# Channel shuffle by tiles: the order of the small tiles at the start and at the end

## Chip, cores, metric

One core of one Trainium2 chip. Times are device microseconds (us) of one execution. Unless said otherwise they are medians of executions in the undisturbed (fast) state. A transfer is issued by an instruction and lands when its completion is signalled. A packet is one record of the trace's DMA view; for the tiles here it is one partition's row, so a tile is 128 packets, 8 on each of 16 DMA engines.

## The reference, cut

```python
def reference(x, groups):                  # x: float32 (16, 64, 64, 256), groups: 8
    b, h, w, c = x.shape
    x = x.reshape(b, h, w, groups, c // groups)
    x = x.transpose(0, 1, 2, 4, 3)         # swap (8, 32) to (32, 8) in each pixel
    return x.reshape(b, h, w, c)
```

65,536 pixels of 1 KB are read and written, 67.11 MB each way. Nothing is computed.

## The kernel before

The pixels are cut into 24 tiles. A tile of q has q KB on each of 128 partitions. Each is loaded, shuffled by one VectorE copy and stored; loads go out on one DMA queue, stores on another.

```python
_SIZES = [4, 4, 8] + [24] * 20 + [16]      # KB a partition
_IN_BUFS = 4
_OUT_BUFS = 4
# ... (pools, flat views of x and out)
    first = 0
    for q in _SIZES:
        in_tile = in_pool.tile([P, biggest * c], F32, name="in_tile")
        nc.sync.dma_start(out=in_tile[:, : q * c], in_=rows(x_flat, first, q))
        out_tile = out_pool.tile([P, biggest * c], F32, name="out_tile")
        nc.vector.tensor_copy(
            out=out_tile[:, : q * c].rearrange("p (i j g) -> p i j g", j=CPG, g=G),
            in_=in_tile[:, : q * c].rearrange("p (i g j) -> p i j g", g=G, j=CPG),
        )
        nc.scalar.dma_start(out=rows(out_flat, first, q), in_=out_tile[:, : q * c])
        first += P * q
```

## Time and profile before

| | before |
|---|---|
| time, first three runs | 317.67 us (317.63 to 317.87) |
| span in the profile | 315.2 us |
| VectorE busy | 122.2 us, 39% |
| rate of both queues, 40 to 280 us | 433 GB/s |

The prediction below shows the page's shares, the rate by stretch and the copies by shape. Two more views of the kernel before belong to the argument. First the DMA issues: transfer, issuing queue, number, KB each, median us from issue to landing.

```profile
in_tile<-in_x_dram SPq DMA_DIRECT2D x20, 3072.0 KB, 52.3
out_dram<-out_tile ACTq DMA_DIRECT2D x20, 3072.0 KB, 40.1
```

A 3 MB transfer alone would need 3.146 MB / 433 GB/s = 7.3 us. These take 52 and 40, so each queue holds several transfers at all times. Second, the end of the chain of waits: start, duration, what.

```profile
244.21 49.91 DMA in_tile<-in_x_dram
...
294.24 3.86 DVE out_tile L49
```

### The profile page before, as it was taken

What the parts mean: (1) busy time and instruction counts of PE and PEld (TensorE: products, weight loads), DVE (VectorE), ACT (ScalarE), POOL (GpSimd) and SP (SyncE); (2) the same over time, 40 slices, a digit from 0 to 9 for tenths busy, and PEclk for the clock granted to TensorE, in tenths of its full rate; (3) what the DMA queues carried; (4) which work ended last, traced back from release to release, by engine and by line L of the source; (5) the groups of instructions that cost most, each with busy time, mean ns of one, the idle gap of its engine ahead of it and who ended that gap; (6) DMA issues with size and microseconds to landing.
All of it is one profiled execution on the core that took longest, in us unless ns stands there. A gap on an engine that the chain in (4) does not pass through costs nothing.

```text
span 315.2 us, 178 instructions
## 1 busy us (share of the span) xinstructions
DVE 122.2 (39%) x24; POOL 0.2 (0%) x4
## 2 busy tenths in 40 slices
DVE  2277517070625335260707162442517070625400
POOL 0000000000000000000000000000000000000000
DMA  8999999999999999999999999999999999999997
GB/s 316 399 458 407 423 424 446 430 421 446 437 415 446 437 418 443 440 415 443 440 415 443 443 412 443 446 409 443 446 415 437 446 415 437 443 420 431 431 437 319
DMA packets 6912, 134.22 MB, mean 426 GB/s; under 512 B 768, under 2 KB 768, under 8 KB 1280
## 3 DMA queue, kind: packets, MB, share of 16 engines
q1 hardware_dynamic: 3456, 67.11, 49.9%
q10 hardware_dynamic: 3456, 67.11, 49.5%
HBM read 67.11 MB, written 67.11 MB: 426 GB/s over the span
## 4 chain that ended last, share of the span: by engine, by line
DMA 38%; another core or an unknown queue 30%; DVE 25%; issue 0%; DVEq 0%
DMA in_tile<-in_x_dram 38%; DVE out_tile L49 25%; DVEq L49 0%
## 5 line engine op out<-in xcount | busy, mean ns | idle before, releaser
L49 DVE COPY out_tile<-in_tile 128x6144 f32<-128x6144 f32 (+3 forms) x24 | 122.2, 5093 | 175.9 <-DMA in_tile<-in_x_dram 175.7
L71 POOL MEMSET const-bfloat16-1.0<- 128x1 bf16 x1 | 0.1, 101 | 0.0
L71 POOL MEMSET const-uint8-127<- 128x1 uint8 x1 | 0.1, 101 | 0.0
L71 POOL MEMSET const-float32-0.0<- 128x1 f32 x1 | 0.1, 98 | 0.2 <-issue 0.2
L71 POOL MEMSET const-float32-1.0<- 128x1 f32 x1 | 0.1, 98 | 0.0
## 6 DMA issues: line engine op xcount, KB each, us to landing
in_tile<-in_x_dram SPq DMA_DIRECT2D x20, 3072.0 KB, 52.3
out_dram<-out_tile ACTq DMA_DIRECT2D x20, 3072.0 KB, 40.1
in_tile<-in_x_dram SPq DMA_DIRECT2D x1, 2048.0 KB, 49.9
out_dram<-out_tile ACTq DMA_DIRECT2D x1, 2048.0 KB, 16.3
in_tile<-in_x_dram SPq DMA_DIRECT2D x2, 512.0 KB, 3.8
in_tile<-in_x_dram SPq DMA_DIRECT2D x1, 1024.0 KB, 6.2
out_dram<-out_tile ACTq DMA_DIRECT2D x2, 512.0 KB, 16.8
out_dram<-out_tile ACTq DMA_DIRECT2D x1, 1024.0 KB, 27.1
```

What stands on the lines that cost most here:

```text
L49: nc.vector.tensor_copy(out=out_tile[:, : q * c].rearrange("p (i j g) -> p i j g", j=CPG, g=G), in_=in_tile[:, : q * c].rearrange("p (i g ...
L71: nc = _bacc.Bacc("TRN2", target_bir_lowering=False, num_devices=1)
```

## The change

The intent is to give the last tile less work after its load (a short copy, a short store), and to grow the first tiles evenly.

```diff
-_SIZES = [4, 4, 8] + [24] * 20 + [16]
+_SIZES = [4, 8, 16] + [24] * 20 + [4]
```

## The prediction

> **What bounds the kernel now.** I read the page first (shares, slices, queues), then the groups by shape, the stretches of DMA rate, the landing times of single transfers, and last the chain. From the page:
>
> ```profile
> span 315.2 us, 178 instructions
> DVE 122.2 (39%) x24; POOL 0.2 (0%) x4
> ...
> DMA  8999999999999999999999999999999999999997
> ...
> DMA packets 6912, 134.22 MB, mean 426 GB/s; under 512 B 768, under 2 KB 768, under 8 KB 1280
> q1 hardware_dynamic: 3456, 67.11, 49.9%
> q10 hardware_dynamic: 3456, 67.11, 49.5%
> ```
>
> VectorE works 39% of the span, the DMA engines all of it but the first and last slice. Queue q1 carries the loads, q10 the stores, 67.11 MB each. How steady that is shows in the busy times by stretch (us, VectorE, POOL, clock, DMA share, GB/s):
>
> ```profile
> 0.00:2.00 2.00, 0.00 (x0) 0.20 (x4) 1.00 0.20 45
> 2.00:8.00 6.00, 2.30 (x3) 0.00 (x0) 1.00 1.05 400
> 8.00:40.00 32.00, 18.32 (x4) 0.00 (x0) 1.00 1.00 422
> 40.00:280.00 240.00, 92.05 (x17) 0.00 (x0) 1.00 1.00 433
> 280.00:294.00 14.00, 5.71 (x1) 0.00 (x0) 1.00 1.00 431
> 294.00:313.00 19.00, 3.86 (x1) 0.00 (x0) 1.00 1.00 432
> 313.00:316.00 3.00, 0.00 (x0) 0.00 (x0) 1.00 0.13 55
> ```
>
> The rate is 433 GB/s with both queues at work (40 to 280) and 432 with stores alone (294 to 313): one ceiling, whoever uses it. 134.22 MB / 0.4327 MB per us = 310.2 us of the 315.2. The five left: 1.73 before the first packet, 1.15 from the last packet (314.08) to the end of the span, and about 2.2 of stalls. Only those 2.2 could depend on this change.
>
> The chain of waits names loads (38%), the copy (25%) and an unknown queue (30%). That is a trap: it follows semaphores, and a load's landing is late because its packets share a full pipe. It also ends at the last copy (298.1) and does not show the 16 us of stores after it. The wait of VectorE for loads (175.7 us) is idle time of an engine that is not the bound.
>
> **What the Trainium skill says.** (1) "DMA: Bandwidth & Descriptors", section "Where 436 GB/s comes from", gives a ceiling of 435.2 GB/s; its warning there lets HBM traffic bind at about 358. The trace has 433 between HBM and SBUF, so here the higher figure binds, and the measurement decides. (2) The same page, "Queues, rings and completion order": each DMA engine takes turns between the rows that have work, packet by packet. The trace agrees, and that is the key to the tail (below). (3) The same page, section "SWDGE vs HWDGE vs iDMA", says packets are preferably at most 4096 B. The packet records here disagree: one packet is one partition's row, 4096 to 24,576 bytes, on both queues.
>
> **The change part by part.** The sizes before are 4, 4, 8, twenty of 24, 16; after 4, 8, 16, twenty of 24, 4. That is the same multiset: one 4 goes from second to last, the 16 from last to third. Nothing is added or removed, 24 loads, 24 copies, 24 stores remain, and so do buffers and waits in kind. Instruction order in the built kernel confirms it. So two sums can't change.
>
> VectorE, from the groups by shape:
>
> ```profile
> L49 DVE COPY out_tile<-in_tile 128x6144 f32<-128x6144 f32 x20 | 114.2, 5708 | 163.7 <-DMA in_tile<-in_x_dram 163.7
> L49 DVE COPY out_tile<-in_tile 128x4096 f32<-128x4096 f32 x1 | 3.9, 3861 | 6.5 <-DMA in_tile<-in_x_dram 6.5
> L49 DVE COPY out_tile<-in_tile 128x1024 f32<-128x1024 f32 x2 | 2.2, 1094 | 4.3 <-DMA in_tile<-in_x_dram 4.1
> L49 DVE COPY out_tile<-in_tile 128x2048 f32<-128x2048 f32 x1 | 2.0, 2019 | 1.4 <-DMA in_tile<-in_x_dram 1.4
> ```
>
> 114.2 + 3.9 + 2.2 + 2.0 = 122.2 us before and after, far under the span.
>
> DMA: undisturbed packets occupy an engine 155 ns for 4 KB, 305 for 8, 607 for 16, 908 for 24 (packet records, start to start). A tile is 128 rows, so 8 packets on each of 16 engines. Per engine and direction: 2 x 8 x 0.155 + 8 x 0.305 + 8 x 0.607 + 160 x 0.908 = 2.48 + 2.44 + 4.86 + 145.28 = 155.06 us; both directions 310.1. Same after.
>
> What does move is who is served when. Because turns go by packet and every tile is 8 packets, loads and stores advance tile for tile, whatever their size. A small packet beside a large one gets a small share. Check on the last load of before, 16 KB packets beside 24 KB stores: 8 x (0.607 + 0.908) = 12.12 us; it landed 12.13 after the load before it. A 4 KB store beside 24 KB loads: 8 x 1.063 = 8.5; the second store landed 8.56 after the first. The lead of loads over stores, counted in packets, is thus fixed when stores begin. Before, the first store was issued at 5.26, its first packet went at 9.29, by when an engine had taken about 26 load packets. When the loads end, 26 store packets per engine remain, 8 of the last tile (16 KB) and 18 of 24 KB: 18 x 0.908 + 8 x 0.607 = 21.2 us. The last load packet ended at 292.86; 292.86 + 21.2 = 314.06, and the last store packet ended at 314.08. The last store's issue and its time from issue to landing show the same queue:
>
> ```profile
> L53 ACTq DMA_DIRECT2D out_dram<-out_tile x1: 338/338/338, 298.1 to 298.1; - x1
> DMA to landing us min/median/max: 16.3/16.3/16.3
> ```
>
> It was issued at 298.1 and landed 16.3 later, of which its own 2.10 MB take 4.86. The copy of 3.86 us before it lay wholly under stores already queued. So before has no exposed tail but the drain itself.
>
> After, start: the first tile is the same, so the first copy ends near 5.2 and the first store is issued near 5.26. By then loads of 4, 8, 16 and 24 KB are queued: 52 KB x 128 = 6.8 MB, 15.8 us of work, against 40 KB and 12.1 us. The fifth load is issued at 5.25 as before. No gap. Load 2 lands near 6.6, its copy (2.02) ends near 8.7; load 3 near 12, its copy (3.86) near 16. Stores take 6.1 us (4 KB beside 16 KB), 9.7 (8 beside 24) and 12.1 (16 beside 24), so each next one is issued before the last is done. Stores begin after about 19 to 21 load packets (estimate: the same four packets, or the same four us, after issue).
>
> After, end: the lead is about 20 packets, not 26. The last load (4 KB packets beside 24 KB stores) takes 8 x 1.063 = 8.5 us. Then 12 store packets of 24 KB and 8 of 4 KB remain: 10.9 + 1.2 = 12.1 us. So the last load lands near 302, its copy of 1.09 ends near 303.5, and the last store, with up to 4 us to its first packet, is ready by 307.5. The stores ahead of it run to about 312.7. It is hidden with 5 us to spare. Sum: path 310.1 before, 310.1 after; difference 0, but for stalls.
>
> Stalls: the packet records show about 0.5 us lost in the first packets, 0.45 at 7 to 9 where loads go to 24 KB packets while no store runs, 0.35 at 31 to 37, and up to 0.7 at the end where the slowest of 16 engines trails the first. The new order may save the second, as stores will run before loads turn to 24 KB. I take 0.2 off, a choice, within what I can't know (0.5 either way). 317.67 - 0.2 = 317.5.
>
> **The rivals.** First, the intended gain: last copy 3.86 to 1.09 and last store 4.86 to 1.24 us, together 6.4, giving 311.3 (just 2% faster). For it: the copy is last in the chain of waits. Against: 16.3 us from issue to landing, so the copy is not exposed, and the bytes taken off the last store are only moved earlier. Second, the tail turns into a new wait: the last load is starved to a seventh of the pipe, the store queue runs dry before it lands, and 1.1 of copy, about 1.4 of issue and receipt (0.73 to 1.73 at the first load, 314.08 to 314.43 at the last store) and 1.2 of store are exposed, 3.7 in all: about 321.4. Against: 12 us of stores should be queued. It would need the lead to fall by more than ten packets. Third, a start that is starved by longer early tiles, or out buffers that come free late: some 2 to 4 us more. Against: the queue of loads is deeper, and the store lag shrinks, so buffers come free earlier. Fourth, small packets being dearer in company: their number is unchanged.
>
> **Range and chances.** Runs of before lie within 0.24 us, and stalls may move by 0.5; so 316.7 to 318.3 holds it 8 times in 10. Within 2% (311.3 to 324.0) is 98%; both sides 1% each, for a rival at its full size.
>
> **What would show it.** Right: 1280 packets under 8 KB again and VectorE at 122.2 us; 432 to 433 GB/s from 40 to past 310; a median landing time of loads still 52.3 us (four tiles of 14.54 less the copy), of stores down from 40.1 to about 31 (20 x 1.816 less 5.8, estimate); the last load landing between 299 and 305, and the last store 8 to 13 us after its issue. Wrong: a dip in the last slices before the last store, or a span that falls by more than 1 us with the same rate. The first would say that the packet lead did not hold; the second that stalls of engines, not bytes, had set the end.

## The result and the profile after

| | before | after |
|---|---|---|
| median of 6 runs | 317.72 us (317.00 to 317.87) | 316.94 us (316.87 to 317.08) |
| span in the profile | 315.2 us | 315.3 us |

The ratio is 0.9979, interval 0.9966 to 0.9992: 0.2% faster. A ratio here is the mean time of one kernel's fast runs over that of the other's of the same rounds, so not quite the ratio of the medians.

The two spans do not show the 0.2%. The profiled execution of before took 317.02 us, as little as the fastest of the six timed ones; that of after took 317.08, the slowest of its six. A profile is one execution; where a kernel scatters, look up which one it was. The experiments take this up.

The page after:

```profile
span 315.3 us, 178 instructions
DVE 122.0 (39%) x24; POOL 0.2 (0%) x4
...
DMA  8999999999999999999999999999999999999997
...
DMA packets 6912, 134.22 MB, mean 426 GB/s; under 512 B 768, under 2 KB 768, under 8 KB 1280
```

The packet line is identical, 1280 under 8 KB included: the multiset of packets has not changed. The stretches after (us, VectorE, POOL, clock, DMA share, GB/s):

```profile
0.00:2.00 2.00, 0.00 (x0) 0.20 (x4) 1.00 0.18 31
2.00:8.00 6.00, 2.44 (x2) 0.00 (x0) 1.00 1.02 410
8.00:40.00 32.00, 15.92 (x4) 0.00 (x0) 1.00 1.01 421
40.00:280.00 240.00, 91.81 (x17) 0.00 (x0) 1.00 1.00 433
280.00:294.00 14.00, 5.12 (x2) 0.00 (x0) 1.00 0.99 427
294.00:313.00 19.00, 6.68 (x2) 0.00 (x0) 1.00 1.00 428
313.00:316.00 3.00, 0.00 (x0) 0.00 (x0) 1.00 0.25 102
```

The pipe is as full as before, start and end included. (The view counts a packet in the stretch where it starts. With its bytes spread over its duration, 280 to 312 us loses 0.05 us, and 0.04 before: 427 and 428 are no dip.) What moved is the order in it. The DMA issues after:

```profile
in_tile<-in_x_dram SPq DMA_DIRECT2D x20, 3072.0 KB, 52.3
out_dram<-out_tile ACTq DMA_DIRECT2D x20, 3072.0 KB, 31.2
```

Loads take as long as before, stores 9 us less, because they begin 5 packets earlier in the order of loads. Nine us of latency less on each of 20 stores, and nothing of it in the time. The end of the chain after:

```profile
256.08 46.27 DMA in_tile<-in_x_dram
...
302.47 1.10 DVE out_tile L49
```

The last copy is 2.8 us shorter and ends 5.5 us later (303.6 against 298.1). The last store after, issue and time to landing:

```profile
L53 ACTq DMA_DIRECT2D out_dram<-out_tile x1: 339/339/339, 303.6 to 303.6; - x1
DMA to landing us min/median/max: 10.9/10.9/10.9
```

It lands 10.9 us after issue, of which its 0.52 MB need 1.24. The rest it waits behind other stores.

### The profile page after: what moved, and what is told of

It is laid out like the page before. It is cut to its first block, busy times and chain, and to the rows that moved or that the text cites. A ratio compares the mean times of both kernels' runs of the same rounds, so it can differ in the third digit from the quotient of the medians.

```text
span 315.3 us, 178 instructions
## 1 busy us (share of the span) xinstructions
DVE 122.0 (39%) x24; POOL 0.2 (0%) x4
## 2 busy tenths in 40 slices
DMA packets 6912, 134.22 MB, mean 426 GB/s; under 512 B 768, under 2 KB 768, under 8 KB 1280
## 4 chain that ended last, share of the span: by engine, by line
DMA 36%; another core or an unknown queue 33%; DVE 26%; SPq 0%; issue 0%; DVEq 0%
DMA in_tile<-in_x_dram 36%; DVE out_tile L49 26%; SPq L47 0%; DVEq L49 0%
## 5 line engine op out<-in xcount | busy, mean ns | idle before, releaser
L49 DVE COPY out_tile<-in_tile 128x6144 f32<-128x6144 f32 (+3 forms) x24 | 122.0, 5082 | 181.6 <-DMA in_tile<-in_x_dram 181.6
## 6 DMA issues: line engine op xcount, KB each, us to landing
in_tile<-in_x_dram SPq DMA_DIRECT2D x20, 3072.0 KB, 52.3
out_dram<-out_tile ACTq DMA_DIRECT2D x20, 3072.0 KB, 31.2
```

The source lines that it names most:

```text
L49: nc.vector.tensor_copy(out=out_tile[:, : q * c].rearrange("p (i j g) -> p i j g", j=CPG, g=G), in_=in_tile[:, : q * c].rearrange("p (i g ...
```

## The experiments

All twelve kernels give the reference's result. Where a stall is sized below ("lost"), it is the length of a stretch less the bytes that the packet records put in it (each packet's spread evenly over its duration) over 432.7 GB/s.

### 1. Is the 0.2% real, and is it the start or the end?

**null_before**: the kernel before, unchanged.

```diff
 (no edit)
```

> The kernel before against itself. Theory (bytes at a fixed rate, the rest small stalls): 317.0 to 317.9 us, ratio 1.000 within 0.001; VectorE 122.2 us; last store 16.3 us from issue to landing. If the run before's two levels (317.0 once, 317.6 to 317.9 otherwise) are chance of one execution, both levels show again, and the 0.2% of the changed kernel is real only if its runs stay at 317.0. Rival: the 0.2% is noise between chips or rounds, then this null ratio leaves 1.000 by about 0.002 as well.

Measured: 317.63 us (317.22 to 317.85, 5 runs), ratio 0.9996 (0.9984 to 1.0009). The null does not leave 1, and three more kernels below repeat the 0.9978 in two rounds; the 0.2% is not noise between rounds. The scatter of 0.6 us is the kernel's own.

**start_only** and **end_only**: one half of the change each.

```diff
-_SIZES = [4, 4, 8] + [24] * 20 + [16]
+_SIZES = [4, 4, 8, 16] + [24] * 20           # start_only
+_SIZES = [4, 8] + [24] * 20 + [16, 4]        # end_only
```

> Sizes 4, 4, 8, 16, twenty of 24: the 16 leaves the end, the 4 stays at the start. Theory: same bytes, same packets, 316.8 to 317.9 us; lead of loads about 27 packets, so the last load lands near 290 and the last store of 24 KB takes about 20 us from issue to landing. Rival (exposed tail): last copy 5.7 instead of 3.9 us and last store 7.3 instead of 4.9, together 4.2 us more, 321.9. Rival (start sets the 0.2%): 317.0 or 317.7 according to whether the stall sits in the second 4 KB tile.

> Sizes 4, 8, twenty of 24, 16, 4: the 4 goes to the end, the 16 stays next to it. Theory: 316.8 to 317.9 us, last load lands 302 to 306, last store hidden behind the 16 KB one. Rival (exposed tail): 2.8 us of copy and 3.6 us of store less, 311.3. Rival (last load starved to a seventh of the pipe and then exposed): 321.4.

Measured: start_only 317.65 us (317.34 to 317.88), ratio 0.9998 (0.9986 to 1.0011); its last load landed at 293.2, three later than expected, its last store took 16.0 from issue to landing where about 20 was expected. The last copy and store were 4.2 us longer in sum than before and the time did not move, against 321.9 for an exposed tail. end_only 316.95 us (316.93 to 317.10), ratio 0.9978 (0.9966 to 0.9991); last load at 306.4, just past the 302 to 306 expected. Not 311.3 and not 321.4. Both rivals about the tail miss by 4 us or more.

But end_only shows the 0.2%. It differs in two things, though: no second 4 KB tile at the start, and 4 KB at the end. So they were crossed, in the next round.

**start_48_end_16** and **start_44_end_8**:

```diff
-_SIZES = [4, 4, 8] + [24] * 20 + [16]
+_SIZES = [4, 8] + [24] * 10 + [4] + [24] * 10 + [16]   # start_48_end_16
+_SIZES = [4, 4, 16] + [24] * 20 + [8]                  # start_44_end_8
```

> Sizes 4, 8, ten of 24, 4, ten of 24, 16: start of the changed kernel, end of the kernel before. The four kernels so far fall in two groups, 316.9 to 317.1 (start 4, 8; last tile 4) and 317.2 to 317.9 (start 4, 4, 8; last tile 16 or 24). Theory S (the start sets it: with two 4 KB tiles first, the third load's first packets stall at 4 to 6 us, where the profile of the repeated kernel before has 227 GB/s against 410 after the change): 316.9 to 317.1, rate of 4 to 6 us near 410. Theory E (the end sets it, the 16 engines end more evenly on 4 KB packets): 317.4 to 317.9.

> Sizes 4, 4, 16, twenty of 24, 8: start of the kernel before, small last tile. Theory S: 317.2 to 317.9 with a scatter of 0.3 us or more between runs, rate of 4 to 6 us well under 400 in a profile of a slow run. Theory E: 316.9 to 317.2 with little scatter.

Measured: start_48_end_16 317.00 us (316.97 to 317.12), ratio 0.9978 (0.9964 to 0.9991). start_44_end_8 317.79 us (317.29 to 318.28), ratio 1.0001 (0.9989 to 1.0014). The start sets it, not the end. The four kernels that begin 4, 8 with nothing else altered in copies or buffers (the changed one, end_only, start_48_end_16, and queue_warm below) have 21 runs within 316.87 to 317.12, whatever tile is last; the three experiments with four buffers that begin 4, 4 with all loads on one queue have 15 runs from 317.22 to 318.28. The kernel before was also run beside each round: with the first six, 33 runs from 317.00 to 318.05, two of which (317.00, 317.09) lie among the fast group. So the start 4, 4, 8 costs about 0.7 us in most executions and next to nothing in a few.

A candidate for what stalls shows from 4 to 6 us, the columns as above (in so short a stretch the last two are rough). The repeated kernel before, in its profiled execution of 317.22 us:

```profile
4.00:6.00 2.00, 1.41 (x2) 0.00 (x0) 1.00 1.09 227
```

The kernel before, in its profiled execution of 317.02 us:

```profile
4.00:6.00 2.00, 1.74 (x2) 0.00 (x0) 1.00 1.05 428
```

The changed kernel:

```profile
4.00:6.00 2.00, 1.10 (x1) 0.00 (x0) 1.00 1.01 410
```

The same program had 227 GB/s here in one execution and 428 in another. In the first, the packet records show the two 4 KB loads through near 4.5 us on most engines, and then the first 8 KB packets of the third load taking 1.1 to 1.7 us on 12 of the 16, where 0.309 is normal: 1.0 us lost from 4 to 6 us. start_only lost 0.43 there in a run of 317.65; its longest 8 KB packet took 0.99, and five took over half as long again as normal. start_44_end_8 lost 0.19 in a run of 317.29, the fastest of its five, so it does not confirm the stall, and my expectation of a rate well under 400 for a slow run stayed untested. The kernels that begin 4, 8 lost 0.07 to 0.12.

This does not yet explain the times. The profile with the 1.0 us stall is of the fastest run of its five, 0.2 us over the run of before that has no stall: it lost less afterwards. By 40 us the profiles of the three 4, 4 experiments had lost 1.9 to 2.1 us in all, those of the four 4, 8 kernels 1.7 to 1.8, that of before 1.6; from 312 us to the last packet all lost 0.2 to 0.7 more, start_only (0.7) the most, as the engines do not end together (its last packets end between 313.6 and 314.7). So the place of the 0.7 us is shown, the start; that it is this stall is not.

The DMA share stays at 1.09 in the stalled stretch: a stalled packet counts as busy. The rate tells, the share doesn't.

**third_load_moved** (third round): sizes as before, the third load issued first on the other queue.

```diff
+    def load(k):                        # cut; the plain loop goes
+        ...
+        queue = nc.scalar if k == 2 else nc.sync
+        queue.dma_start(out=tiles[k][:, : q * c], in_=rows(x_flat, firsts[k], q))
+
+    for k in range(_IN_BUFS):
+        load(k)          # the first four loads ahead of all stores
```

> The kernel before (sizes unchanged) with the third load (8 KB) issued first on the queue that issues the stores, so it does not stand behind the two 4 KB loads. If the 0.7 us of the start order 4, 4, 8 come from that load not being ready when the first 1.05 MB are through: 316.9 to 317.2, scatter under 0.25. If they come from anything else of that start (the second small store, the issue of two loads and two stores between 5.2 and 6.5 us): 317.3 to 317.9 with scatter as before.

Measured: 317.13 us (317.09 to 317.17), ratio 0.9984 (0.9971 to 0.9997). The scatter is gone and most of the 0.7 us with it, as expected if a third load that comes late behind 1.05 MB of short tiles is the cause. Its rate:

```profile
2.00:4.00 2.00, 0.00 (x0) 0.00 (x0) 1.00 0.80 244
4.00:6.00 2.00, 0.00 (x0) 0.00 (x0) 1.00 1.05 438
```

The start with two queues is slower at first (244 GB/s from 2 to 4 us), which may be why 0.15 to 0.2 us are left. The edit changes more of the start than that: the first copy starts at 6.84 us and not 4.12, the first store's first packet goes at 11.5 and not 9.3. So this supports the explanation and does not prove it. Why the third load is late in some executions only, and whether that makes the slow ones, stays open; a profile of a run near 317.8 would tell.

### 2. Is the last copy hidden, and by how much?

**last_copy_x6** and **last_copy_x13**: the changed kernel, with the last tile's copy repeated.

```diff
-        nc.vector.tensor_copy(
+        for _ in range(13 if first + P * q == b * h * w else 1):   # 6 in last_copy_x6
+            nc.vector.tensor_copy(
```

> The changed kernel with the last tile's copy done 6 times over, 5 x 1.09 = 5.5 us more before the last store. In the changed kernel the last store is issued at 303.60 and, with 1.24 us of its own before its landing at 314.49, sends its first packet near 312.3; with 1.0 us from issue to packet the slack is 7.7 us. Theory (last copy hidden): 316.9, within 0.3 us. Rival (exposed tail): 322.4.

> The same with 13 copies, 12 x 1.09 = 13.1 us more, which is 5.4 more than the slack of 7.7. Theory: 322.3, between 321.3 and 323.3, with the DMA engines idle for about 5 us before the last store. Rival (exposed tail): 330.0. If the last packets queue for longer after issue (as the first store did, 3.9 us), 325.

Measured: last_copy_x13 322.31 us (322.28 to 322.52), 5.37 over the changed kernel. The trace has the last store issued 13.4 us later than in the changed kernel (a copy and the gap after it take 1.12) and its first packet 5.6 us later, so 7.8 were hidden, close to the 7.7 worked out. last_copy_x6 317.40 us (317.35 to 317.62): 5.5 us added, 0.46 seen, 0.16 more than expected. Its span is 315.2, as in the changed kernel (315.3), so the 0.46 lie outside the span that the profile covers; where, I can't say. Inside the span the copies cost nothing. The end of last_copy_x13:

```profile
310.00:313.00 3.00, 2.90 (x4) 0.00 (x0) 1.00 0.63 270
313.00:316.00 3.00, 2.90 (x4) 0.00 (x0) 1.00 0.00 0
316.00:321.00 5.00, 0.98 (x1) 0.00 (x0) 1.00 0.26 105
```

This is what an exposed tail looks like: VectorE busy and 0 GB/s from 313 to 316. Neither the kernel before nor the changed one has such a stretch.

### 3. Why do the first stores start late?

**queue_warm**: the changed kernel, with a small load first on the stores' queue.

```diff
+    warm_tile = warm_pool.tile([P, 64], F32, name="warm_tile")
+    nc.scalar.dma_start(out=warm_tile, in_=rows(x_flat, 0, 1)[:, :64])
```

> The changed kernel with a 32 KB load into a scratch tile put first on the queue that issues the stores. In both traces the first store is issued at 5.26 and sends its first packet at 9.2 to 9.3, 3.9 us later, where the first load needs 1.0. Theory A (first use of that queue costs about 3 us): here the first store packet goes near 6.3, the lead falls to about 13 packets, store latency from 31 to about 23 us, and the last load lands 4 to 6 us later than the 302.4 of the changed kernel. Theory B (delay is the store waiting behind prefetched load packets or its write path): still near 9.2. For the time both expect 316.7 to 317.3; if the sag of 7 to 10 us (about 0.45 us lost) is the missing stores' doing, A takes 0.3 off.

Measured: 316.93 us (316.89 to 317.09), ratio to the kernel before 0.9978 (0.9964 to 0.9991). The first store still sent its first packet at 9.4 us, its last load landed at 302.2, its stores took a median of 30.5 us. Theory A is out. The first store of queue_warm took 12.0 us from issue to landing, that of the changed kernel 12.6. Two traces speak for the waiting behind loads that theory B names first: the last store of last_copy_x13, issued with nothing else under way, sent its first packet 0.84 us after issue, and in experiment 5, with three loads issued before it and not four, the first store's delay was 2.1 and 2.4 us. How queued loads hold a store up for four us, when later the two take turns packet by packet, stays open.

### 4. Is a small first tile needed?

**two_sizes**: no small tile at the start at all.

```diff
-_SIZES = [4, 4, 8] + [24] * 20 + [16]
+_SIZES = [24] * 21 + [8]
```

> Twenty-one tiles of 24 KB, then one of 8: no small first tile at all. The first copy starts near 9 and ends near 15 instead of 5.2 us, stores begin ten us later. Theory (bytes; the pipe does not care whether loads or stores fill it): 316.5 to 317.3, with only loads up to 16 to 19 us at 400 GB/s or more. Rival (a small first tile is needed to start the stores early): 10 us more of unpaired time, 322 or more. If loads alone with 24 KB packets run slower than the mix (363 GB/s at 8 us before), 318 to 319.

Measured: 317.41 us (317.25 to 317.63), ratio to before 0.9993 (0.9980 to 1.0006); just above the 316.5 to 317.3 of the theory, far from 322. The first store packet comes 12 us later (21.2 against 9.3) and the time is that of the kernel before. The rate of two_sizes:

```profile
4.00:16.00 12.00, 4.83 (x1) 0.00 (x0) 1.00 1.01 434
16.00:22.00 6.00, 4.38 (x2) 0.00 (x0) 1.00 0.99 377
```

Loads alone, in 24 KB packets, run at 434 GB/s from 4 to 16 us. So 24 KB loads without a store beside them do not sag by themselves, as I had thought. The sag lies at 16 to 22, between the first store's issue (16.9) and its first packet (21.2), as the sag of 7 to 10 us in the kernels before and after lies near the beginning of theirs. That is not general: in third_load_moved the loads turned to 24 KB packets at 7.4 us and the first store packet went at 11.5, and it lost 0.06 us from 6 to 12 and 0.06 from 12 to 14. So neither the turn to 24 KB packets nor the beginning of the stores brings the sag by itself; its cause stays open.

### 5. When would the order matter?

**before_two_bufs** and **after_two_bufs**: both kernels with half the buffers.

```diff
-_IN_BUFS = 4
-_OUT_BUFS = 4
+_IN_BUFS = 2
+_OUT_BUFS = 2
```

> The kernel before with 2 input and 2 output buffers instead of 4 and 4. Theory (the order costs nothing only while load and store queues never run dry together): here the third load must wait for the first copy (5.25 us, plus 1.0 to its first packet = 6.3) while the two 4 KB loads are through at 4.3: about 2 us of idle pipe; and the copies wait for output buffers behind the slow small stores, another 1.5 to 2.5 us between 15 and 22 us. 320 to 322.5. If nothing but bytes counts, 317.6.

> The changed kernel with 2 and 2 buffers. Theory: the loads of 4 and 8 KB last until 5.5, so about 0.8 us idle before the third, and the larger early tiles leave no second gap: 317.0 to 318.3, so 2 to 5 us under the kernel before with the same buffers. If bytes alone count: 317.0. If the small last load (served one packet in two beside 24 KB stores) is exposed by the shorter store queue: 320 or more.

Measured: before_two_bufs four runs of 318.92, 323.64, 324.84 and 343.55; the last two count as slow, being over 1.5% above the fastest (the median of all four is 324.24). after_two_bufs 318.56 us (317.93 to 319.15). The fast runs against the kernel before with four buffers: 1.0115 (1.0045 to 1.0185) and 1.0032 (1.0013 to 1.0052). The difference of 0.8% between the orders rests on two runs of before_two_bufs, and the intervals overlap: that the new order is faster here is likely, but not shown. The start of before_two_bufs, in its run of 318.92:

```profile
4.00:6.00 2.00, 1.86 (x2) 0.00 (x0) 1.00 0.33 123
6.00:8.00 2.00, 0.23 (x1) 0.00 (x0) 1.00 0.94 215
```

And of after_two_bufs:

```profile
4.00:6.00 2.00, 1.09 (x1) 0.00 (x0) 1.00 0.85 356
6.00:8.00 2.00, 1.54 (x1) 0.00 (x0) 1.00 0.98 260
```

The first gap is the expected one: the DMA engines are idle (share 0.33) until the third load, issued after the first copy, sends its packets; 1.4 us lost from 4 to 6 us, against 0.2 in the new order. From 6 to 8 us both lose about 1.1 more, so in the new order the gap is shorter (1.4 against 2.5 in all) but not the 0.8 expected. The second gap, at 15 to 22 us, did not appear in this run: the first store went out 2.1 us after issue, not 3.9, perhaps because fewer loads stood in the engines' way. So the profiled run is 1 us under the expected range; after_two_bufs is 0.3 us over its own. What costs 5 us and more in the other runs, none of which was profiled, stays open.

## Why the prediction was right

**Bytes bound.** It predicted 317.5 (316.7 to 318.3) with hardly any movement; measured 316.94. The step that carries it, the same packets at the same rate, is shown by the identical packet line, 433 GB/s in both and VectorE at 122.0 against 122.2 us.

**Turns by packet, and the lead.** It put the lead of loads over stores at 19 to 21 packets instead of 26: 21 in the records. It put the last load near 302 (302.35), the end of its copy near 303.5 (303.56), the last store 8 to 13 us from issue to landing (10.9), the loads' median at 52.3 (52.3) and the stores' near 31 (31.2).

**The rivals.** The exposed tail (311.3) and the starved last load (321.4) fell by end_only and start_only. The slack behind the second is 7.8 us by last_copy_x13; the prediction had "5 us to spare" with a delay of up to 4 us at the first packet (0.84 in last_copy_x13). The third rival, a start or buffers that cost 2 to 4 us more, and the fourth, dearer small packets, do not show: the changed kernel is not slower.

**The stalls: the size in range, the reason wrong.** The 0.2 us off were chosen for the stall at 7 to 9 us, "as stores will run before loads turn to 24 KB". They did: the first store packet went at 9.2, the first 24 KB load packet at 11.9 (9.3 and 7.1 in before). But nothing was saved by it. From 6 to 12 us the changed kernel lost 0.49 us, the kernel before 0.53; the stall fell on the 16 KB packets of the third load (up to 1.01 us at 8 to 10, where 0.607 is normal), and two_sizes and third_load_moved show that 24 KB loads without a store beside them need not sag. The step that failed is that this stall comes of loads going to 24 KB packets with no store running, and would go. The gain of 0.7 us instead sits, by the crossed experiments, in the start 4, 4, 8; a late third load behind two 4 KB tiles, seen clearly in one profile and weakly in another, is the candidate and is not shown to be the cause. That the sign came out right, and that the range of 0.8 us either way held the result, was luck as far as this term goes. A hint of a loss that comes and goes was there to be weighed: the profiled run took 317.02 us, and the three timed ones 317.63 to 317.87. The statement that runs of before lie within 0.24 us held for those three, not for the six (0.87).

## What to carry to other kernels

Where one shared pipe is full from start to end, reordering the same transfers moves latencies and waits, and hardly time: count bytes and packets first, then only the stretches in which the rate falls. A copy or store at the end of a chain of waits is worth nothing while other transfers are queued ahead of it; work out that queue, or lengthen the last step until it shows, and you have the slack. Judge differences under 1% from several executions and not from two profiles: a profile can show a stall of 1 us and still be of a fast run.

## What the Trainium skill lacked or had wrong

- "DMA: Bandwidth & Descriptors", section "Where 436 GB/s comes from": its warning lets HBM traffic bind at about 358 GB/s, half of a stack's rate; that this holds with both cores of a domain streaming stands only in the note under the same page's table of measured rates. Here, on one core, reads and writes of HBM together ran at 433 from 40 to 280 us, near its figure for the fabric (435.2).
- The same page, section "Queues, rings and completion order": turns by packet agree with the records, but not said is what follows for tiles of different row size: a 0.52 MB load beside 24 KB stores landed 8.5 us after the load before it, 61 GB/s of 433.
- No page that I read: the bytes of a packet on the two queues used here. All packets of the tiles were whole partition rows, up to 24,576 B (0.908 us on an engine, against 0.155 for 4096 B).
- No page that I read: the start of the stores beside queued loads. The first packet of the first store went 3.6 to 4.4 us after issue with four loads or more issued before it, also after an earlier transfer on that queue (4.1), and 2.1 and 2.4 us with three; that of a last store with nothing else under way went after 0.84 us.
- No page that I read: the third load's first packets taking 1.1 to 1.7 us instead of 0.31 on 12 of 16 engines, in one profiled execution of the kernel before and not in the other, after two loads of 0.52 MB. Cause open.
